# Block pairs of a two-layer DiT feed-forward: another layout of the weight tile, one split for A11 and A12, and another order of sums and products

## The chip, the core and the metric

The kernel runs on one core of one Trainium2 chip. The metric is the device time of one execution in microseconds. Each kernel is run several times and the median counts; differences are judged between kernels that ran on the same chip.

## The reference, cut to what matters

The reference is a two-layer diffusion transformer on 256 latent tokens and 256 context tokens with 1024 channels, all in float32. Layer 0 mixes with a short convolution, layer 1 with grouped-query attention. Around each mixer stand two gated feed-forwards. Each is this, on normalised and modulated tokens `h`, with a hidden size of 2816:

```python
def _swiglu(h, w13, w2):
    gte, up = jnp.split(h @ w13, 2, axis=-1)
    return (jax.nn.silu(gte) * up) @ w2
...
lat = lat + 0.5 * mod[:, 0, 2] * _swiglu(_modulate(lat, ...), ffn_w13[i, 0], ffn_w2[i, 0])
if cx is not None:
    cx = cx + 0.5 * modc[0, 2] * _swiglu(_modulate(cx, ...), ffn_w13[i, 0], ffn_w2[i, 0])
```

The first three of the four feed-forwards, (layer, place) = (0, 0), (0, 1) and (1, 0), run over both token streams; the last, (1, 1), over the latent stream alone. The change touches the product `h @ w13` of the first three.

## The kernel before

**Numbers.** TensorE works on float32r, and every operand is split into a high part and a low part. `split` (lines 107 to 109) does it with two operations: ScalarE copies the source into the high part with rounding (L108), VectorE subtracts that from the source for the low part (L109). `mm3` (lines 133 to 139) then adds three matmuls: high by high (L137), high weight by low token (L138), low weight by high token (L139).

**Tokens.** Activations lie transposed: 128 channels on the partitions, 512 columns, of which the first 256 are the latent and the last 256 the context tokens.

**Thirds.** The hidden size is cut into 22 tiles of 128, and these into thirds of 8, 7 and 7 (line 23). For each third, `ffn` (lines 777 to 886) makes the gated hidden tiles, and `project` (lines 584 to 643) multiplies them by `w2` and adds the result to the residual `x` (L567). The last two hidden tiles of a third are finished in between the first products of the projection.

**Pairs.** Most hidden tiles are computed by a `Pair` (lines 691 to 775), the Winograd form of Strassen's product: 7 block products in place of 8. The weight of one hidden tile is a 2 by 2 matrix of blocks of 128 rows by 512 columns: A11 and A12 are the gate's halves along the channels, A21 and A22 the up-projection's. The tokens are blocks B, by half of the channels and by stream. Sums of the B blocks are T1 to T4 (`Blocks.sums`, lines 412 to 432), made once for each feed-forward. Sums of the weights are made for each pair:

- S1 = A21 - A22, S2 = A11 - S1, S3 = A22 - S2 (which is A21 - A11), S4 = A12 - S2.

A product of one block, `prod` (lines 740 to 743), is 4 times `mm3`, so 12 matmuls of 256 columns. The seven are A11 with B11 and A12 with B21 (`head`), S1 with T1 (`five`), S2 with T2 and S4 with B22 (`six`), S3 with T3 (`seven`) and A22 with T4 (`four`). They are added up in two PSUM tiles, `p` and `q`. ScalarE copies `p` after A11 (L751), `q`'s second half after S1 (L757) and `p` after S2 (L761). VectorE then adds `sg` from `q` (L763), ScalarE applies Silu (L764), VectorE adds into `u` (L768), multiplies to the gate product `gm` (L774), and `gm` is split into the hidden tile `gh`, `gl`.

**Weights of a pair.** The DRAM tile `w13` has 2048 columns in four blocks of 512, in the order A21, A11, A22, A12 (lines 1432 and 1433). SyncE loads the last two blocks into the raw tile `r2`, and A11 into the second half of `r1`. GpSimd writes the negative of A22 into the first half of `r1` (L704), and a DMA issued by GpSimd adds A21 there (L707), so that `r1` holds S1 and A11. A11 is split from `r1` and A12 from `r2`, 512 columns each (L712). VectorE subtracts within `r1` (L726), and `keep` splits S1 and S2 at once, 1024 columns. Then A22 is split off by `split_far` (lines 111 to 115): two operations on ScalarE (L113, L114), and a DMA of GpSimd that adds the source to the negative high part. VectorE subtracts S2 from both halves of `r2` at once (L734, the wide sum), and S3 and S4 are split together.

**Buffers.** Raw tiles have 8 buffers (`wr`), split tiles 4 for each part (`wh`, `wl`), A22's parts 2 each (`w4h`, `w4l`).

**Order.** Nobody writes the order of these stages by hand (only the start of the kernel and the attention heads are): a scheduler orders the instructions of each engine from the order of the calls, the buffers and its own estimates. Between the pairs, VectorE also computes the modulation vectors, one row product of 1024 columns at a time (L178), doled out by `tick`. The products of the former pair's S3 and A22 come among those of the next pair. On TensorE the order in the middle of a third is A11, A12, S1, S3 of the former pair, S2, S4, A22 of the former pair. There are 56 pairs: 16 in (0, 0), whose first six tiles are computed plainly, and 20 each in (0, 1) and (1, 0), whose first two are.

Of the kernel before, what the change touches and what calls it, by code (L numbers as in the profile page):

```python
# [10 lines left out]
F32R = mybir.dt.float32r  # L11
# [5 lines left out]
P = 128  # L17
# [5 lines left out]
THIRDS = (8, 7, 7)  # L23

AS_IS = {(0, 0): range(3, 6), (0, 1): (), (1, 0): ()}

EARLY = 4
HEADS = 8
# [19 lines left out]
def hybrid_kernel(ctx: ExitStack, tc: tile.TileContext, a: dict, out: bass.AP):  # L48
# [68 lines left out]
    def half():  # L117

        return tuple(
            wp.tile([P, 1024], F32R, name=nm(t), tag=t, bufs=4) for t in ("wh", "wl")  # L120
        )
# [569 lines left out]
    class Pair:  # L691
# [6 lines left out]
        def __init__(self, src, h):  # L698
            self.h, self.w, self.src = h, {}, src
            r2 = load_raw(src[:, 1024:2048])  # L700
            r1 = wp.tile([P, 1024], F32, name=nm("wr"), tag="wr", bufs=8)
            nc.sync.dma_start(r1[:, T2:], src[:, T2:1024])

            nc.gpsimd.tensor_scalar(  # L704
                out=r1[:, :T2], in0=r2[:, :T2], scalar1=-1.0, scalar2=None, op0=ALU.mult
            )
            nc.gpsimd.dma_start(out=r1[:, :T2], in_=src[:, :T2], accum_op=ALU.add)  # L707
            self.raw = [r1, r2]
            ts = half()
            for i, key in enumerate(("A11", "A12")):  # L710
                self.w[key] = [t[:, i * T2 : i * T2 + T2] for t in ts]
                split(*self.w[key], self.raw[i][:, T2:])  # L712

        def keep(self, keys, part):
            hi, lo = half()
# [4 lines left out]
        def sums(self, n):  # L720

            r1, r2 = self.raw
            s1, s2 = r1[:, :T2], r1[:, T2:]
            tt = nc.vector.tensor_tensor
            if n == 0:
                tt(out=s2, in0=s2, in1=s1, op=ALU.subtract)  # L726
                self.keep(("S1", "S2"), r1)
                return
            self.w["A22"] = [
                wp.tile([P, T2], F32R, name=nm(t), tag=t, bufs=2) for t in ("w4h", "w4l")  # L730
            ]
            split_far(*self.w["A22"], r2[:, :T2], self.src[:, 1024 : 1024 + T2])
            v = lambda t: t.rearrange("p (a c) -> p a c", a=2)
            tt(  # L734
                out=v(r2), in0=v(r2), in1=s2.unsqueeze(1).to_broadcast([P, 2, T2]),
                op=ALU.subtract,
            )
            self.keep(("S3", "S4"), r2)

        def prod(self, ps, wk, hk, first=True):  # L740
            for k in range(4):
# [14 lines left out]
            self.gm = tp.tile([P, T2], F32, name=nm("gm"), tag="gm", bufs=3)  # L756
            nc.scalar.copy(self.gm[:, S:], self.q1)  # L757

        def six(self):
            self.prod(self.p, "S2", "T2", False)  # L760
            nc.scalar.copy(self.sg[:, S:], self.p)  # L761
            self.prod(self.q1, "S4", ("B", 1, 1), False)
            nc.vector.tensor_tensor(out=self.sg, in0=self.q, in1=self.sg, op=ALU.add)  # L763
            nc.scalar.activation(out=self.sg, in_=self.sg, func=AF.Silu)  # L764
# [12 lines left out]
    def ffn(l, b, h, tot, gate, tail, gs=(), ev=(0, 0), z=None):  # L777
        gs = list(gs)
        i0 = 0
        for t, n in enumerate(THIRDS):  # L780
            between = ()
            if tot == T2:
                heads = []
                if t == 0 and not gs:

                    w = [load_w(a["w13"][l, b, 0])]
                    gs = [new_pair("g") for _ in range(2)]
                    pp = [(psum("pg"), psum("pu")) for _ in range(2)]
                    w13_mm(pp[0], w[0], h, range(KT), 0, S)
                    flush()  # L790
                    w.append(load_w(a["w13"][l, b, 1]))
                    with tc.issue_after(every[-1]):
                        w13_mm(pp[1], w[1], h, range(KT), 0, S)
                    h.sums(0)
                    w13_mm(pp[0], w[0], h, range(KT), S, T2)
                    w13_post(pp[0], gs[0], 0, T2)
                    heads.append(Pair(a["w13"][l, b, 2], h))
                    h.sums(1)
                    heads[0].sums(0)
                    w13_mm(pp[1], w[1], h, range(KT), S, T2)  # L800
                    w13_post(pp[1], gs[1], 0, T2)
                    heads[0].head()
                    h.sums(2)
                    heads[0].sums(1)
                prev = None
                for i in range(len(gs), n):
                    if t == 0 and not heads and i in AS_IS[l, b]:
                        w = load_w(a["w13"][l, b, i])
                        pp = psum("pg"), psum("pu")
                        if prev:  # L810
                            prev.seven()
                        if "T1" not in h.t:
                            with tc.issue_after(rows["W1"]):
                                h.sums()
                        w13_mm(pp, w, h, range(4), 0, T2)
                        if prev:
                            gs.append(new_pair("g"))
                            prev.four(gs[-1])
                            prev = None
                        w13_mm(pp, w, h, range(4, KT), 0, T2)  # L820
                        gs.append(new_pair("g"))
                        tick(3, w13_post(pp, gs[-1], 0, T2))
                        continue
                    if heads:
                        pr = heads.pop(0)
                    else:
                        pr = Pair(a["w13"][l, b, i0 + i], h)
                        pr.sums(0)
                        pr.sums(1)
                        pr.head()  # L830
                    pr.five()
                    at = prev.seven().ins if prev else None
                    pr.six()
                    if prev:
                        gs.append(new_pair("g"))
                        prev.four(gs[-1])
                    prev = pr
                    if i:
                        tick(0.9, at)

                def last():
                    gs.append(new_pair("g"))
                    prev.four(gs[-1])

                between = (prev.seven, last) if prev else ()
            else:
                for i in range(n):
                    w = load_w(a["w13"][l, b, i0 + i])
                    gs.append(beside(gp.tile([P, T2], F32R, name=nm("gx"), tag="gh")))
                    pp = psum("pg"), psum("pu")  # L850
                    if i0 + i < EARLY:
                        for k in range(KT):
                            for j in range(2):
                                ps = pp[j][:, : z.w]
                                mm3(ps, w(at13(1 - j, k)), z.at(k), k == 0, k == KT - 1)
                            if i == 0 and k == KT // 2:
                                flush(1)
                        if i < 3:
                            flush(1)
                        early_post(pp, gs[i], z.ri)  # L860
                        tick(1)
                        continue
                    for j in range(2):
                        ws = [w(at13(1 - j, k)) for k in range(KT)]
                        mm_wide(pp[j], ws, [h.both(k) for k in range(KT)], True, True)
                    beside_post(pp, gs[i])
                    tick(1)
            i0 += n

            def ws2(m):  # L870
                src = a["w2a"][l, b, m // 2] if t == 0 else a["w2b"][l, b, t - 1, m // 2]
                o = (m % 2) * n * P
                raw = load_raw(src[:, o : o + n * P], n * P)
                hi, lo = half()
                split(hi[:, : n * P], lo[:, : n * P], raw[:, : n * P])
                return lambda k: (hi[:, k * P : k * P + P], lo[:, k * P : k * P + P])

            cur = gs
            end = t == len(THIRDS) - 1
            project(  # L880
                ws2,
                (lambda k, c0, c1: cur[k]) if tot == S
                else lambda k, c0, c1: (cur[k][0][:, c0:c1], cur[k][1][:, c0:c1]), n,
                gate, tail if end else None, tot, 2 if end and tot == T2 else 0, ev[end], between,
            )
            gs = []
# [525 lines left out]
def _layout(inp):  # L1412
# [17 lines left out]
    d["modb"] = f("mod_b").reshape(2, 72, P).transpose(2, 0, 1)  # L1430
    d["normg"] = f("norm_g").reshape(2, 3, KT, P).transpose(3, 0, 1, 2)
    w13 = f("ffn_w13").reshape(2, 2, 2, KT // 2, P, 2, NM, P)[:, :, :, :, :, ::-1]
    d["w13"] = w13.transpose(0, 1, 6, 4, 2, 5, 3, 7).reshape(2, 2, NM, P, 2048)
    w2 = f("ffn_w2").reshape(2, 2, NM, P, KT // 2, 2, P)
    w2 = w2.transpose(0, 1, 4, 3, 5, 2, 6)
    n0, n1 = THIRDS[:2]
# [53 lines left out]
```

## Time and profile before

| what | value |
|---|---|
| median of 3 runs | 1559.67 us |
| lowest and highest run | 1559.26 and 1561.86 us |
| span of the profiled execution, first to last instruction | 1558.7 us |
| VectorE operations, splits (L109) among them | 2030, 446 |
| ScalarE operations, splits (L108) among them | 1297, 446 |
| GpSimd operations | 187 |
| mean granted TensorE clock | 1.000 |

The time of the profiled execution is not listed apart from its span; the span lies 0.97 us below the median of the runs, which also hold what lies before the first and behind the last instruction. In the rows of a profile, PE is TensorE's matmul, PEld its weight load, DVE is VectorE, ACT ScalarE, POOL GpSimd and SP SyncE. A row of the timeline has start, length, engine, line, operation, tiles out and in, shape and count, and in brackets the idle time before it with what ended that. Rows that follow each other with the same line and tiles are merged, so the start of the next row tells how far apart operations start: an engine begins the next one before the former has fully ended.

### The profile page before, as it was taken

Reading aid. Unit: us, or ns where it says so; the run is one execution under the profiler, and the core shown is the slowest. Engines: PE = TensorE matmul, PEld = TensorE weight load, DVE = VectorE, ACT = ScalarE, POOL = GpSimd, SP = SyncE. Lnnn points to the kernel's source line nnn. Section 1 sums busy time; section 2 is a strip of 40 time slices with the busy share of each in tenths; the row PEclk is TensorE's granted clock in tenths of the full one; section 3 lists DMA queues with packets and bytes.
Section 4 is the critical chain, followed back from the end, with each engine's and each line's share of the span. In section 5 each row is a group of like instructions: output and inputs, shape, how many; then the busy total and the mean of one; then the engine's idle time right before and its main releaser. Section 6 shows DMA issues by size and latency. Waiting matters only on the chain.

```text
span 1558.7 us, 26399 instructions
## 1 busy us (share of the span) xinstructions
PE 1549.9 (99%) x10296; PEld 1422.0 (91%) x10296; DVE 1281.7 (82%) x2030; ACT 782.1 (50%) x1297; POOL 221.6 (14%) x187
## 2 busy tenths in 40 slices
PE   9999999999999999999999999999999999999999
PEld 7898998999888899989999899989999898998888
DVE  5788789799987588968978888968978887888676
ACT  5642553644423366436346466436346455774553
POOL 0012213200000112032042112022042002300000
PEclk9999999999999999999999999999999999999999
DMA  9567467465555425655656635655766843276562
GB/s 371 194 173 200 109 191 193 120 194 161 191 198 178 115 62 136 205 146 130 206 144 158 200 71 136 203 149 130 235 170 170 264 156 114 93 234 219 172 197 74
DMA packets 88253, 263.53 MB, mean 169 GB/s; under 512 B 10816, under 2 KB 12608, under 8 KB 88128
## 3 DMA queue, kind: packets, MB, share of 16 engines
q1 hardware_dynamic: 69408, 230.72, 45.8%
q0 software_dynamic: 16128, 29.37, 11.3%
q10 hardware_dynamic: 2592, 1.76, 0.4%
q8 instruction: 80, 1.31, 0.3%
q14 instruction: 45, 0.37, 0.1%
HBM read 259.45 MB, written 1.05 MB: 167 GB/s over the span
## 4 chain that ended last, share of the span: by engine, by line
PE 96%; DVE 2%; ACT 1%; issue 0%; POOL 0%; DVEq 0%; ACTq 0%; POOLq 0%
PE py L137 9%; PE py L138 9%; PE py L139 9%; PE p L137 7%; PE p L139 7%; PE p L138 7%; PE q L137 5%; PE q L139 5%; PE q L138 5%; PE py L145 2%; PE pu L145 2%; PE pg L145 2%; PE py L147 1%; PE pg L147 1%; PE pu L147 1%; PE pv L138 1%
## 5 line engine op out<-in xcount | busy, mean ns | idle before, releaser
L108 ACT ACTIVATE wh<-wr 128x1024 fp32r<-128x1024 f32 (+2 forms) x446 | 394.5, 912 | 325.2 <-PE py L138 126.1
L109 DVE TENSOR_TENSOR wl<-wr,wh 128x1024 fp32r<-128x1024 f32 (+2 forms) x446 | 456.6, 1048 | 85.9 <-ACT wh L108 66.8
L178 DVE CUSTOM_DVE_ANT_0 junk<-wr,scbc,modb 128x1024 bf16<-128x1024 f32 x213 | 274.7, 1290 | 11.4 <-DMA wr<-in_modT 9.3
L137 PE MATMUL py<-gh,wh 128*128 128x512 f32 (+1 forms) x570 | 213.5, 375 | 0.0
L138 PE MATMUL py<-gl,wh 128*128 128x512 f32 (+1 forms) x570 | 213.3, 374 | 0.0
L139 PE MATMUL py<-gh,wl 128*128 128x512 f32 (+1 forms) x570 | 213.2, 374 | 0.0
L704 POOL TENSOR_SCALAR wr<-wr 128x512 f32<-128x512 f32 x56 | 101.1, 1805 | 541.7 <-DMA wr<-in_w 286.3
L567 DVE SCALAR_TENSOR_TENSOR x<-py,mod,x 128x256 f32<-128x256 f32 x213 | 94.6, 479 | 65.6 <-PE py L139 54.3
L138 PE MATMUL p<-tl,wh 128*128 128x256 f32 x448 | 126.9, 283 | 0.0
L139 PE MATMUL p<-th,wl 128*128 128x256 f32 x448 | 126.9, 283 | 0.0
L137 PE MATMUL p<-th,wh 128*128 128x256 f32 x448 | 126.9, 283 | 0.0
L139 PEld LDWEIGHTS py<-gh,wl 128*128 128x128 f32 x570 | 107.4, 188 | 19.2
L137 PEld LDWEIGHTS py<-gh,wh 128*128 128x128 f32 x570 | 107.5, 189 | 18.3
L138 PEld LDWEIGHTS py<-gl,wh 128*128 128x128 f32 x570 | 107.5, 189 | 17.9
L115 POOL DMA_DIRECT2D w4l<-in_w x56 | 53.8, 960 | 445.7 <-ACT w4l L114 431.9
L137 PE MATMUL q<-bh,wh 128*128 128x256 f32 x320 | 90.8, 284 | 0.8 <-ACT wh L108 0.8
L139 PE MATMUL q<-bh,wl 128*128 128x256 f32 x320 | 90.8, 284 | 0.0
L138 PE MATMUL q<-bl,wh 128*128 128x256 f32 x320 | 90.6, 283 | 0.0
L137 PEld LDWEIGHTS p<-th,wh 128*128 128x128 f32 x448 | 86.0, 192 | 0.3
L138 PEld LDWEIGHTS p<-tl,wh 128*128 128x128 f32 x448 | 86.0, 192 | 0.3
L139 PEld LDWEIGHTS p<-th,wl 128*128 128x128 f32 x448 | 86.1, 192 | 0.0
L764 ACT ACTIVATE sg<-sg 128x512 f32<-128x512 f32 x56 | 35.4, 632 | 90.8 <-DVE sg L763 90.6
(305 smaller groups left out, 4081.2 us busy)
## 6 DMA issues: line engine op xcount, KB each, us to landing
wr<-in_w SPq DMA_DIRECT2D x120, 512.0 KB, 4.8
wr<-in_modT SPq DMA_DIRECT2D x117, 512.0 KB, 4.9
wr<-in_w2b SPq DMA_DIRECT2D x64, 448.0 KB, 4.0
wr<-in_w2a SPq DMA_DIRECT2D x32, 512.0 KB, 4.6
wr<-in_w SPq DMA_DIRECT2D x56, 256.0 KB, 3.9
wr<-in_w POOLq DMA_DIRECT2D x56, 256.0 KB, 5.8
w4l<-in_w POOLq DMA_DIRECT2D x56, 256.0 KB, 5.9
pm<-in_mod SPq DMA_DIRECT2D x16, 512.0 KB, 10.2
```

Source lines behind the costliest of these rows:

```text
L108: nc.scalar.activation(out=hi, in_=src, func=AF.Copy)
L109: return nc.vector.tensor_tensor(out=lo, in0=src, in1=hi.bitcast(F32), op=ALU.subtract)
L115: nc.gpsimd.dma_start(out=lo, in_=src, accum_op=ALU.add)
L137: nc.tensor.matmul(ps, wh, mh, start=first, stop=False, **kw)
L138: nc.tensor.matmul(ps, wh, ml, start=False, stop=False, **kw)
L139: nc.tensor.matmul(ps, wl, mh, start=False, stop=last, **kw)
L145: nc.tensor.matmul(ps, w[0], m[2], start=first and n == 0, stop=False)
L147: nc.tensor.matmul(ps[:, :S], w[1], m[0], start=False, stop=last and n == len(ms) - 1)
L178: nc.vector.tensor_tensor_reduce(out=junk, in0=raw, in1=scbc[:, v, :], scale=0.5 if ch in (2, 8) else 1.0, scalar=modb[:, l, col : col + 1 ...
L567: ins = nc.vector.scalar_tensor_tensor(out=x[:, m, s * S : s * S + S], in0=ps[:, o : o + S], scalar=g[:, m, s : s + 1], in1=x[:, m, s * S ...
L704: nc.gpsimd.tensor_scalar(out=r1[:, :T2], in0=r2[:, :T2], scalar1=-1.0, scalar2=None, op0=ALU.mult)
L764: nc.scalar.activation(out=self.sg, in_=self.sg, func=AF.Silu)
```

## The change

The four blocks of a pair's weight tile lie as A21, A22, A11, A12, for the tiles that are computed by pairs (the new table `SINGLE` tells from which tile on). So `r2` holds A11 and A12, which `keep` splits in one operation of 1024 columns. `r1` holds A21 - A11, which is S3, and A22. The first sum is now S2 = A22 - S3; A22 is split off before it, since the sum overwrites it; S3 and S2 are split together. The wide sum gives S1 = A11 - S2 and S4 = A12 - S2, and these are split together. The products are called in another order: S2 (`two`), S3 of the former pair, S1, A22 of the former pair, S4.

```diff
+SINGLE = {(0, 0): 6, (0, 1): 2, (1, 0): 2}
...
             nc.gpsimd.dma_start(out=r1[:, :T2], in_=src[:, :T2], accum_op=ALU.add)
             self.raw = [r1, r2]
-            ts = half()
-            for i, key in enumerate(("A11", "A12")):
-                self.w[key] = [t[:, i * T2 : i * T2 + T2] for t in ts]
-                split(*self.w[key], self.raw[i][:, T2:])
+            self.keep(("A11", "A12"), r2)
...
         def sums(self, n):
             r1, r2 = self.raw
-            s1, s2 = r1[:, :T2], r1[:, T2:]
+            s2 = r1[:, T2:]
             tt = nc.vector.tensor_tensor
             if n == 0:
-                tt(out=s2, in0=s2, in1=s1, op=ALU.subtract)
-                self.keep(("S1", "S2"), r1)
+                self.w["A22"] = [
+                    wp.tile([P, T2], F32R, name=nm(t), tag=t, bufs=2) for t in ("w4h", "w4l")
+                ]
+                split_far(*self.w["A22"], s2, self.src[:, T2:1024])
+                tt(out=s2, in0=s2, in1=r1[:, :T2], op=ALU.subtract)
+                self.keep(("S3", "S2"), r1)
                 return
-            self.w["A22"] = [
-                wp.tile([P, T2], F32R, name=nm(t), tag=t, bufs=2) for t in ("w4h", "w4l")
-            ]
-            split_far(*self.w["A22"], r2[:, :T2], self.src[:, 1024 : 1024 + T2])
             v = lambda t: t.rearrange("p (a c) -> p a c", a=2)
             tt(
                 out=v(r2), in0=v(r2), in1=s2.unsqueeze(1).to_broadcast([P, 2, T2]),
                 op=ALU.subtract,
             )
-            self.keep(("S3", "S4"), r2)
+            self.keep(("S1", "S4"), r2)
...
-        def six(self):
+        def two(self):
             self.prod(self.p, "S2", "T2", False)
             nc.scalar.copy(self.sg[:, S:], self.p)
+
+        def six(self):
             self.prod(self.q1, "S4", ("B", 1, 1), False)
...
+                    pr.two()
+                    at = prev.seven().ins if prev else None
                     pr.five()
-                    at = prev.seven().ins if prev else None
-                    pr.six()
                     if prev:
                         gs.append(new_pair("g"))
                         prev.four(gs[-1])
+                    pr.six()
...
-    d["w13"] = w13.transpose(0, 1, 6, 4, 2, 5, 3, 7).reshape(2, 2, NM, P, 2048)
+    w13 = w13.transpose(0, 1, 6, 4, 2, 5, 3, 7).reshape(2, 2, NM, P, 4, 512).copy()
+    for (l, b), n in SINGLE.items():
+        w13[l, b, n:] = w13[l, b, n:, :, (0, 2, 1, 3)].transpose(1, 2, 0, 3)
+    d["w13"] = w13.reshape(2, 2, NM, P, 2048)
```

## The prediction

> **What bounds the kernel now.** I read the page first: spans of the engines, the clock, and the chain that ended last.
>
> ```profile
> span 1558.7 us, 26399 instructions
> PE 1549.9 (99%) x10296; PEld 1422.0 (91%) x10296; DVE 1281.7 (82%) x2030; ACT 782.1 (50%) x1297; POOL 221.6 (14%) x187
> PEclk9999999999999999999999999999999999999999
> PE 96%; DVE 2%; ACT 1%; issue 0%; POOL 0%; DVEq 0%; ACTq 0%; POOLq 0%
> ```
>
> TensorE is busy for 99% of the span at full granted clock, and 96% of the chain is its own work. So time saved on VectorE or ScalarE is worth nothing where TensorE has its operands, and a new wait of TensorE costs its full length. Next I read a stretch inside the block pairs: busy time by engine, then the timeline of TensorE and of its weight loads.
>
> ```profile
> 602.00:642.00 40.00, 40.00 (x336) 40.00 (x335) 35.63 (x47) 26.11 (x44) 9.30 (x8) 1.00 0.64 170
> ```
>
> ```profile
> 602.00 0.28 PE L139 MATMUL p<-th,w4l 128*128 128x256 f32 x1
> 602.12 0.28 PE L137 MATMUL p<-bh,wh 128*128 128x256 f32 x1
> 602.36 0.28 PE L139 MATMUL p<-bh,wl 128*128 128x256 f32 x1
> 612.20 0.28 PE L137 MATMUL p<-bh,wh 128*128 128x256 f32 x1
> ```
>
> ```profile
> 602.25 0.19 PEld L139 LDWEIGHTS p<-bh,wl 128*128 128x128 f32 x1
> ```
>
> The columns of the first row are length, then busy us (and instructions) of PE, PEld, DVE, ACT, POOL, the clock, DMA. One pair is 7 products of 12 matmuls. From the first matmul of A11 at 602.12 to the next pair's at 612.20 are 84 matmuls in 10.08 us: 0.12 us each, with no gap. A weight load starts 0.11 us ahead of its matmul (602.25 for 602.36), so weights that land later than that stop TensorE.
>
> **Why nothing stops it today.** The same loop on VectorE, and the product that uses the weights:
>
> ```profile
> 618.07 0.68 DVE L726 TENSOR_TENSOR wr<-wr 128x512 f32<-128x512 f32 x1
> 620.21 1.22 DVE L109 TENSOR_TENSOR wl<-wr,wh 128x1024 fp32r<-128x1024 f32 x1
> 622.49 0.69 DVE L774 TENSOR_TENSOR gm<-sg,p 128x512 f32<-128x512 f32 x1 [0.46 <-PE p L139]
> 623.32 1.22 DVE L734 TENSOR_TENSOR wr<-wr,wr 128x1024 f32<-128x1024 f32 x1
> 624.46 0.68 DVE L109 TENSOR_TENSOR gl<-gm,gh 128x512 fp32r<-128x512 f32 x1
> ```
>
> ```profile
> 622.16 0.28 PE L139 MATMUL p<-th,w4l 128*128 128x256 f32 x1
> 625.16 0.28 PE L137 MATMUL q<-th,wh 128*128 128x256 f32 x1
> ```
>
> The S1, S2 weights of the pair whose A11 starts at 622.28 are complete at 621.43 and first used at 625.16: 3.7 us to spare. Their sum (L726) does not wait for the gate product: it runs before L774.
>
> **The change, part by part.** (1) The merged split. 56 times two splits of 512 columns become one of 1024.
>
> ```profile
> L109 DVE TENSOR_TENSOR wl<-wr,wh 128x512 fp32r<-128x512 f32 x132 | 86.0, 690 | 12.4 <-ACT wh L108 12.1
> L109 DVE TENSOR_TENSOR wl<-wr,wh 128x1024 fp32r<-128x1024 f32 x250 | 304.9, 1228 | 68.1 <-ACT wh L108 54.7 <-ACT sg L671 9.5 <-PE pu L147 3.1
> L108 ACT ACTIVATE wh<-wr 128x512 fp32r<-128x512 f32 x132 | 75.8, 620 | 29.8 <-PE py L138 24.4 <-PE q L138 2.5 <-PE pu L138 2.2
> L108 ACT ACTIVATE wh<-wr 128x1024 fp32r<-128x1024 f32 x250 | 263.1, 1058 | 231.2 <-PE py L138 72.8 <-DVE wr L726 51.7 <-PE p L138 27.6
> ```
>
> By these means VectorE saves 56 x (2 x 690 - 1228) ns = 8.5 us and ScalarE 56 x (2 x 620 - 1058) = 10.2 us. In the loop both had idle time (35.6 and 26.1 of 40 us busy), and TensorE hides all of it: 0.
>
> (2) The new order, in the loop. The instructions of the built changed program stand on VectorE, 38 times, as: GM (the gate product, old L774), the S2 sum, the wide sum, gl, SG (old L763), the low part of S3/S2, of S1/S4, of the next A11/A12, U (old L768), a modulation unit. On TensorE: A11, A12, two matmuls of S2, five of the former pair's S3, the other ten and seven, S1, A22 of the former pair, S4. The 38 are pairs 3 to 7 of six thirds with seven pairs and pairs 3 to 6 of the two with six; others have their sums made earlier, in the projection. GM waits for the former pair's A22 product, and the new pair's S2 weights now stand behind GM in VectorE's queue. That is the new chain; its rows:
>
> ```profile
> 642.14 0.69 DVE L763 TENSOR_TENSOR sg<-q,sg 128x512 f32<-128x512 f32 x1
> 642.74 0.68 DVE L774 TENSOR_TENSOR gm<-sg,p 128x512 f32<-128x512 f32 x1
> ```
>
> ```profile
> 674.82 0.68 DVE L726 TENSOR_TENSOR wr<-wr 128x512 f32<-128x512 f32 x1
> 675.60 1.23 DVE L734 TENSOR_TENSOR wr<-wr,wr 128x1024 f32<-128x1024 f32 x1
> ```
>
> ```profile
> 588.87 1.06 ACT L108 ACTIVATE wh<-wr 128x1024 fp32r<-128x1024 f32 x1 [0.37 <-DVE wr L734]
> 589.98 0.19 PEld L137 LDWEIGHTS q<-bh,wh 128*128 128x128 f32 x1 [0.66 <-ACT wh L108]
> ```
>
> Counted from the start of the last A22 matmul: 0.33 until GM starts (622.16 to 622.49); 0.60 to the next 512-column operation (642.14 to 642.74); S2 sum 0.78 to the wide sum, which needs its result (674.82 to 675.60); wide sum 1.14 (623.32 to 624.46); gl 0.60; SG 0.60; low part 1.22; 0.05 from an engine's end to the weight load (589.93 to 589.98). Sum 5.32 us. TensorE meanwhile has 12 + 24 + 2 + 5 matmuls; the 44th is S2's third, the first with a low part: 44 x 0.12 - 0.11 = 5.17. It is late by 0.15 us, each time: 38 x 0.15 = **5.7 us**. The lateness closes on itself: it delays the next A22 product as much.
>
> ScalarE's side is shorter: behind the wide sum (ended at 0.33 + 0.60 + 0.78 + 1.23 = 2.94) the high part of S1/S4, 1.06, the copy that frees A11's sum in PSUM for S2, 0.37, and 0.05 make 4.42, against 37 x 0.12 - 0.11 = 4.33 for S2's first matmul: late by 0.09, inside the 0.15. The S2 sum also waits, newly, for the high part of A22 on ScalarE, which waits for the second-last A22 matmul (two w4 buffers). At 0.62 us, as the 512-column row above, it runs from 0.20 to 0.82, and GM keeps VectorE until 0.93: 0. Were that cover gone, each 0.1 us would cost 38 x 0.1 = 3.8. Behind a late S2 sum stands VectorE's whole list, so both split halves; U, the next that TensorE waits for (at the former pair's A22), keeps some 0.7 us by the same rows.
>
> (3) Where a pair opens a third, S4 now follows S1 with only four matmuls between (before, S2's twelve). Both use one PSUM half, and ScalarE's copy stands between.
>
> ```profile
> 616.40 0.28 PE L139 MATMUL q<-th,wl 128*128 128x256 f32 x1
> 616.72 0.37 ACT L757 COPY gm<-q 128x256 f32<-128x256 f32 x1
> ```
>
> From S1's last matmul: 0.32 to the copy, 0.37, 0.05 = 0.74; S4's first load is due at 5 x 0.12 - 0.11 = 0.49. Late by 0.25, nine times: **2.2 us**.
>
> (4) Two stalls go. At the start of the second and third feed-forward VectorE is late with the wide sum, and S4 waits:
>
> ```profile
> 589.24 0.28 PE L139 MATMUL p<-th,wl 128*128 128x256 f32 x1
> 593.72 0.28 PE L137 MATMUL q<-bh,wh 128*128 128x256 f32 x1
> ```
>
> ```profile
> 939.66 0.28 PE L139 MATMUL p<-th,wl 128*128 128x256 f32 x1
> 944.08 0.28 PE L137 MATMUL q<-bh,wh 128*128 128x256 f32 x1
> ```
>
> 27 matmuls lie between, 3.24 us; they took 4.48 and 4.42: 1.24 + 1.18 = 2.4 us of stall. In the changed order the wide sum stands third from T1's low part on, not fourteenth. What is late next?
>
> ```profile
> 575.46 1.22 DVE L109 TENSOR_TENSOR tl<-hr,th 128x1024 fp32r<-128x1024 f32 x1
> ```
>
> ```profile
> 587.92 0.28 PE L137 MATMUL p<-th,wh 128*128 128x256 f32 x1
> ```
>
> From 575.46, eight operations of 1024 columns at 1.14, three of 512 at 0.60 and its own 1.22 end the low part of S1/S4 at 587.60. S1, now in the place that S2 has at 587.92, loads it at 587.92 + 0.24 - 0.11 = 588.05. So **-2.4 us**; one more 1024-column operation ahead would put 0.7 us of each stall back.
>
> (5) The queues. POOL and SP issue the same list; what moves is the release of raw tile r1, now behind the low part of S3/S2 (3.7 us into a pair's time, by the sum above).
>
> ```profile
> 611.94 2.27 POOL L704 TENSOR_SCALAR wr<-wr 128x512 f32<-128x512 f32 x1 [4.13 <-DVE sg L763]
> 614.62 0.89 POOL L707 DMA_DIRECT2D wr<-in_w  x1 [0.41 <-POOL wr L704]
> ```
>
> ```profile
> wr<-in_w POOLq DMA_DIRECT2D x56, 256.0 KB, 5.8
> ```
>
> POOL's negation, its issue and the landing take 2.3 + 0.9 + 5.8 = 9.0 us. The tile serves the pair two later, whose S2 sum starts 9.4 into the pair between: 10.1 - 3.7 + 9.4 = 15.8. With 6.8 us to spare, 0.
>
> Sum: 5.7 + 2.2 - 2.4 = 5.5 us on the profiled span of 1558.7, so 1564.2; the median of the runs shown, 1559.67, lies 0.97 above that span, so **1565.2 us**.
>
> **Bounds.** Lateness per loop, as an estimate from these rows: 0 if the dependent sum starts like an independent one (0.60, not 0.78), and 0.46 if the longest wide sum fell into every chain:
>
> ```profile
> L734 DVE TENSOR_TENSOR wr<-wr,wr x56: 1214/1225/1533, 85.4 to 1206.4; 128x1024 f32<-128x1024 f32 x56
> ```
>
> That is 1.53 against 1.22 (minimum, median and maximum in ns). I take 0.15, the sum of the common rows.
>
> **Rivals.** *Covered, and not slower.* If the wide sum follows the S2 sum as closely as an independent operation, the chain is 5.14 against 5.17, and no loop stalls: 1559.67 + 2.2 - 2.4 = 1559.5; with the copy in (3) hidden too, 1557.3. It decides at 0.15 us of a 5.3 us chain. Against it stands the pair at 674.82, where the second starts 0.10 after the first ends. The Trainium skill speaks for it ("VectorE: DVE Perf Modes", section "The DRAIN you can't avoid"): a semaphore between chained operations costs nothing extra. The trace disagrees by that pair's 0.18 us. Chance 0.22.
>
> *Heavier.* Lateness 0.46 per loop gives 17.5 + 2.2 - 2.4: 1577.0. For it speaks that the chain has no slack to take a stretched row; against it, that the median wide sum is within 0.01 us of the shortest, and that VectorE's loop, about 8.8 of 10.2 us by these rows, has its idle time ahead of GM, where extra work falls. Chance 0.12.
>
> *It does not do what it says.* The built program has 56 fewer splits on both engines; no chance left.
>
> **How the numbers follow.** Forecast 0.66, with its own range 1561.5 to 1570. The range of 1559.0 to 1574.0 takes in most of the covered case and stops short of the heavier one. 0.2% (3.1 us) is about what a measurement of this kernel can tell from no change. Faster than 1556.6 lies beyond even the best covered time: 0.03. Within 0.2%: 0.19 from covered and 0.03 from the forecast's low end, 0.22. Slower: 0.75.
>
> **What would show it.** In the changed profile: pairs 10.2 us apart in the loop; weight loads of p at S2 waiting for VectorE's low part some 38 times; nine waits of q at S4 for the ScalarE copy; no wait near 589 and 940. If pairs stay 10.08 us apart, step (2) is wrong; if they are 10.4 or more apart, its size is.

## The result, and the profile after

| what | before | after |
|---|---|---|
| median of the runs on the same chip | 1560.2 us (4 runs, 1559.26 to 1561.86) | 1578.03 us (4 runs, 1576.23 to 1579.72) |
| ratio, with its 95% interval | | 1.0114 (1.0102 to 1.0125) |
| span of the profiled execution | 1558.7 us | 1574.5 us |
| time of the profiled execution | | 1576.23 us |

The changed kernel is slower by 17.8 us, where 5.5 were forecast. The profiled execution is the fastest of the four; its span grew by 15.8 us, and that is what the trace can account for. All lines of the changed kernel up to the pairs have moved down by two (L109 is L111), the S2 sum is L729, the wide sum L733, the gate product GM L775. First the page: span, busy times, and the chain that ended last.

```profile
span 1574.5 us, 26263 instructions
...
PE 1560.4 (99%) x10296; PEld 1428.1 (91%) x10296; DVE 1279.4 (81%) x1974; ACT 775.3 (49%) x1241; POOL 227.1 (14%) x187
...
PE 90%; DVE 3%; DMA 3%; ACT 1%; issue 1%; POOL 1%; ACTq 0%; SPq 0%; POOLq 0%; DVEq 0%
```

The 56 splits are gone from VectorE (1974 operations for 2030) and ScalarE (1241 for 1297), and TensorE still reads 99%. But the chain is TensorE's own work for 90% only, not 96%, and 3% of it are now a DMA, which had no share at all. So something that waits for a transfer has come onto the path. The waits of TensorE's weight loads and of VectorE (columns: who waited, for whom, us in total, times, longest) say where:

```profile
PEld ss L277 <- DVE acc L268: 4.4, 2, 3.6
PEld p L139 <- ACT sg L750: 3.0, 8, 1.1
...
PEld q L139 <- ACT gm L756: 1.7, 9, 0.2
```

```profile
DVE gm L775 <- PE p L141: 49.0, 38, 2.4
...
DVE wr L729 <- DMA wr<-in_w: 26.1, 9, 5.1
```

The nine waits of `q` for ScalarE's copy and the 38 of GM for the A22 product were forecast. The two waits of the RMS sum (`ss`, L277) and the 26.1 us in which VectorE stood at an S2 sum for a transfer were not. Before, VectorE stood there 4.5 us in two places:

```profile
DVE wr L726 <- DMA wr<-in_w: 4.5, 2, 3.5
```

**Where the 15.8 us are.** Matmuls of one form start at a usual distance (0.12 us for 256 columns, 0.227 for 512). I summed from TensorE's records, place by place, by how much they start farther apart. The same sums of four experiments below stand beside it:

| us beyond the usual distance | before | after | e1_heads | e2_w4h | e7_fill15 | e8_all2 |
|---|---|---|---|---|---|---|
| first 60 us | 13.8 | 12.4 | 13.5 | 13.4 | 12.9 | 13.7 |
| pairs, products into `p` | 0.4 | 8.5 | 10.0 | 1.0 | 8.0 | 2.1 |
| pairs, products into `q` | 1.8 | 2.1 | 2.1 | 2.2 | 2.1 | 0.7 |
| ahead of the second feed-forward, 545 to 575 us | 0.1 | 6.3 | 0.1 | 5.7 | 0.9 | 0.1 |
| ahead of the third, 895 to 926 us | 1.4 | 3.1 | 2.3 | 4.0 | 3.1 | 1.6 |
| rest up to 1240 us | 0.7 | 1.5 | 0.7 | 5.5 | 0.7 | 0.7 |
| behind 1240 us | 4.4 | 4.4 | 4.3 | 4.3 | 5.0 | 4.4 |
| sum | 22.6 | 38.3 | 33.0 | 36.2 | 32.7 | 23.2 |

(In e7_fill15 come 3.4 us of dummy matmuls on top.) The difference of the first two sums is 15.7 of the span's 15.8 us: +8.0 in the pairs' loops, +0.3 at S4, and +7.9 ahead of the second and third feed-forward, about which the prediction said nothing; 0.8 came in small pieces, and the first 60 us, which the change does not touch, were 1.4 us shorter in this execution (all rounded).

**The part that was not foreseen.** VectorE in the changed kernel, at the end of the projection ahead of the second feed-forward (start, length, engine, line, operation, tiles; in brackets the idle time before it and what ended that):

```profile
550.51 0.76 DVE L268 TENSOR_TENSOR acc<-acc,sq 128x256 f32<-128x256 f32 x2
556.35 0.69 DVE L729 TENSOR_TENSOR wr<-wr 128x512 f32<-128x512 f32 x1 [5.08 <-DMA wr<-in_w]
556.96 0.48 DVE L569 SCALAR_TENSOR_TENSOR x<-py,mod,x 128x256 f32<-128x256 f32 x1
557.91 0.43 DVE L268 TENSOR_TENSOR acc<-acc,sq 128x256 f32<-128x256 f32 x1 [0.48 <-ACT sq L260]
```

```profile
548.77 1.49 POOL L706 TENSOR_SCALAR wr<-wr 128x512 f32<-128x512 f32 x1 [6.74 <-DVE wl L111]
550.66 0.91 POOL L709 DMA_DIRECT2D wr<-in_w  x1 [0.41 <-POOL wr L706]
```

```profile
558.40 0.59 PE L277 MATMUL ss<-ones,acc 128*128 128x1 f32 x2 [3.37 <-DVE acc L268]
```

Read it from the S2 sum at 556.35. It belongs to the second pair of the next feed-forward. VectorE came to it at 551.27 and stood for 5.08 us, since the transfer that completes raw tile `r1` was issued by GpSimd only at 550.66. Behind it in VectorE's order stand the last residual `x` (L569) and the square sum `acc` (L268), which have nothing to do with the weights. TensorE needs `acc` for the RMS sum, and stood for 3.4 us. Before, no L726 runs between 535 and 566 us; the first head pair's sum ran at 578.94, behind the norm, and stood for no transfer there. Stretches of the changed kernel's TensorE from there (length, busy us and count of PE, PEld, DVE, ACT, POOL, then the granted clock, DMA share and GB/s):

```profile
555.00:558.00 3.00, 0.02 (x1) 0.00 (x0) 1.17 (x3) 0.42 (x1) 0.00 (x0) 0.84 0.66 113
558.00:560.00 2.00, 1.35 (x6) 1.27 (x6) 0.74 (x2) 0.42 (x1) 0.00 (x0) 0.50 0.00 0
560.00:562.00 2.00, 2.00 (x11) 2.00 (x11) 0.17 (x1) 0.26 (x1) 0.00 (x0) 0.50 0.00 0
562.00:564.00 2.00, 2.00 (x11) 2.00 (x11) 1.15 (x3) 0.64 (x2) 0.00 (x0) 0.53 0.00 0
564.00:566.00 2.00, 2.00 (x19) 2.00 (x18) 2.00 (x6) 2.00 (x6) 0.00 (x0) 1.00 0.00 0
```

The busy share says 2.00 of 2 us from 560 to 564, but only 11 matmuls ran in each stretch, against 19 from 564 on: the granted clock had dropped to 0.50. So the stop cost 3.5 us, 0.5 at the second square sum, and 2.3 more at half pace.

### The profile page after: what moved, and what is told of

It is laid out like the page before. It is cut to its first block, busy times and chain, and to the rows that moved or that the text cites. A ratio compares the mean times of both kernels' runs of the same rounds, so it can differ in the third digit from the quotient of the medians.

```text
span 1574.5 us, 26263 instructions
## 1 busy us (share of the span) xinstructions
PE 1560.4 (99%) x10296; PEld 1428.1 (91%) x10296; DVE 1279.4 (81%) x1974; ACT 775.3 (49%) x1241; POOL 227.1 (14%) x187
## 4 chain that ended last, share of the span: by engine, by line
PE 90%; DVE 3%; DMA 3%; ACT 1%; issue 1%; POOL 1%; ACTq 0%; SPq 0%; POOLq 0%; DVEq 0%
PE py L139 7%; PE py L140 7%; PE py L141 7%; PE p L139 7%; PE p L141 7%; PE p L140 7%; PE q L139 5%; PE q L140 5%; PE q L141 5%; DMA wr<-in_w 3%; PE py L147 2%; PE pu L147 2%; PE pg L147 2%; PE py L149 1%; PE pg L149 1%
## 5 line engine op out<-in xcount | busy, mean ns | idle before, releaser
L111 DVE TENSOR_TENSOR wl<-wr,wh 128x1024 fp32r<-128x1024 f32 (+2 forms) x390 | 453.1, 1184 | 58.4 <-ACT wh L110 39.4
L706 POOL TENSOR_SCALAR wr<-wr 128x512 f32<-128x512 f32 x56 | 105.0, 1874 | 756.6 <-DMA wr<-in_w 353.9
L569 DVE SCALAR_TENSOR_TENSOR x<-py,mod,x 128x256 f32<-128x256 f32 x213 | 94.4, 478 | 41.7 <-PE py L141 30.5
L141 PEld LDWEIGHTS p<-th,wl 128*128 128x128 f32 x448 | 82.6, 191 | 1.4
L775 DVE TENSOR_TENSOR gm<-sg,p 128x512 f32<-128x512 f32 x56 | 38.5, 687 | 49.0 <-PE p L141 49.0
```

What stands on the lines that cost most here:

```text
L111: return nc.vector.tensor_tensor(out=lo, in0=src, in1=hi.bitcast(F32), op=ALU.subtract)
L141: nc.tensor.matmul(ps, wl, mh, start=False, stop=last, **kw)
L569: ins = nc.vector.scalar_tensor_tensor(out=x[:, m, s * S : s * S + S], in0=ps[:, o : o + S], scalar=g[:, m, s : s + 1], in1=x[:, m, s * S ...
L706: nc.gpsimd.tensor_scalar(out=r1[:, :T2], in0=r2[:, :T2], scalar1=-1.0, scalar2=None, op0=ALU.mult)
L775: nc.vector.tensor_tensor(out=self.gm, in0=self.sg, in1=self.u, op=ALU.mult)
```

## The experiments

All are edits of the changed kernel. Each was run on one chip together with the kernel before, whose median there was 1559.9 to 1560.1 us; the ratios are to that. The theory: three separate losses, the head sums' wait in VectorE's order (7.9 us), the chain through GM in the loop (8.0), the copy ahead of S4 (2.2). The rivals: another cause of the late RMS sum, a VectorE that is too full in any order, a clock that drops for another reason.

### e1_heads: the head pairs' S2 sums behind the norm

`recs` holds the reciprocals of the norm, one for each stream. On the engines exactly these four sums move, and nothing else.

```diff
             if n == 0:
...
-                tt(out=s2, in0=s2, in1=r1[:, :T2], op=ALU.subtract)
+                with tc.issue_after(at) if at else nullcontext():
+                    self.sum = tt(out=s2, in0=s2, in1=r1[:, :T2], op=ALU.subtract).ins
...
-                    heads[0].sums(0)
+                    heads[0].sums(0, recs[-2])
...
-                        pr.sums(0)
+                        pr.sums(0, recs[-1] if t == 0 and i == 3 and (l, b) != (0, 0) else None)
```

> The changed kernel, with the first weight sum (S2) of the first two pairs of the second and third feed-forward put behind the two reciprocals of the norm on VectorE, out of the projection before it; no other instruction moves. Theory H (VectorE stands at these sums and waits for the transfer that completes raw tile r1, and the residual and the square sums queue behind it): the 3.5 us wait of the RMS sum near 555 and the half-speed stretch behind it go, and most of the wait near 913; of the changed kernel's 1578 us some 7.5 go, so 1570.5 (1569 to 1572). Rival (the RMS sum is late because the squares or the transfers of that moment are slow): the wait stays where it is, 1577 to 1579.

Measured: 1570.09 us (5 runs, 1567.67 to 1571.98), ratio to before 1.0063 (1.0050 to 1.0075). That is 7.9 us less than the changed kernel. VectorE at the same place:

```profile
551.76 0.48 DVE L569 SCALAR_TENSOR_TENSOR x<-py,mod,x 128x256 f32<-128x256 f32 x1
552.89 0.43 DVE L268 TENSOR_TENSOR acc<-acc,sq 128x256 f32<-128x256 f32 x1 [0.64 <-ACT sq L260]
...
557.17 0.17 DVE L286 RECIPROCAL ri<-rs 128x2 f32<-128x2 f32 x1 [2.04 <-ACT rs L282]
557.25 0.69 DVE L730 TENSOR_TENSOR wr<-wr 128x512 f32<-128x512 f32 x1
```

The square sum ends at 553.3 in place of 558.3, the S2 sum (now L730) fits behind the reciprocal without any wait, and TensorE loses 0.1 us from 545 to 575 in place of 6.3. (The spans differ by 5.3 us only: the changed kernel's profiled execution is its fastest, and 1.5 us came in the pairs, with one wait of 1.9 us from 1158.3 to 1160.3, ahead of which VectorE stands at the first two S2 sums of the last third for their transfers.) The transfers were left as they were, so it was the place of the sum in VectorE's order, and not a slow transfer by itself. The S1 weights were not late afterwards either: what the prediction feared behind the norm did not happen.

### e2_w4h: a third buffer for A22's high part

```diff
-                    wp.tile([P, T2], F32R, name=nm(t), tag=t, bufs=2) for t in ("w4h", "w4l")
+                    wp.tile([P, T2], F32R, name=nm(t), tag=t, bufs=n) for t, n in (("w4h", 3), ("w4l", 2))
```

(The edit also gives GM's method an argument that no call uses.)

> The changed kernel with three buffers in place of two for the high part of A22, so that the S2 sum of the next pair no longer waits for the former pair's A22 product. Theory L (the chain A22 product, GM, S2 sum, wide sum, low part of S3/S2 is what stops TensorE by 0.17 us in each of 38 loops, and by up to 0.4 in one loop of each third): pairs come 10.08 us apart again and some 8 us go, 1570 (1568.5 to 1571.5). Rival (VectorE is simply too full in the loop, in whichever order): pairs stay at 10.2 us and the time at 1577 to 1579.

Measured: 1574.98 us (4 runs, 1574.11 to 1575.10), ratio 1.0094 (1.0080 to 1.0107); a miss in the time, 3.1 us where 8 were expected. The place by place sums show why. In the loop it came as expected: `p` loses 1.0 us in place of 8.5, and VectorE's waits for the A22 product have nearly gone, from 38 to 3:

```profile
DVE gm L776 <- PE p L141: 2.0, 3, 0.7
```

A pair takes the usual time again:

```profile
628.83 0.28 PE L139 MATMUL p<-bh,wh 128*128 128x256 f32 x1
...
638.90 0.28 PE L139 MATMUL p<-bh,wh 128*128 128x256 f32 x1
```

10.07 us lie between the starts of two pairs. So VectorE is not too full: the order was the limit. (The edit lets the scheduler change the order in many places on every engine, so it tests the order as a whole and not one wait. In the loop of the changed kernel at 628, A22's rounding on ScalarE, which needs the buffer, ended at 628.75, and VectorE went from GM to the S2 sum at 628.85: both held that sum, nearly equally.) But with a buffer more the scheduler pulled further S2 sums forward, at the head of the third feed-forward too, and these now stand ahead of the norm's scaling (L307):

```profile
930.60 0.69 DVE L729 TENSOR_TENSOR wr<-wr 128x512 f32<-128x512 f32 x1 [2.73 <-issue]
931.21 1.65 DVE L307 SCALAR_TENSOR_TENSOR t<-x,A,ss 128x256 f32<-128x256 f32 x4
```

```profile
933.37 0.39 PE L139 MATMUL pg<-bh,wh 128*128 128x256 f32 x1 [1.06 <-ACT bh L110]
...
935.18 0.58 PE L140 MATMUL pg<-bl,wh 128*128 128x256 f32 x1 [1.07 <-DVE bl L111]
```

TensorE waited there twice for the scaled tokens and ran at half pace behind it. This is the loss that e1_heads removes, in a new place. The line "rest" of the table holds it: 5.5 us in place of 1.5, so 4.0 of the 7.5 us won in the pairs were given back.

### e3_third: S1 before S2 where a pair opens a third

```diff
-                    pr.two()
-                    at = prev.seven().ins if prev else None
-                    pr.five()
+                    if prev or (t == 0 and i == 2):
+                        pr.two()
+                        at = prev.seven().ins if prev else None
+                        pr.five()
+                    else:
+                        pr.five()
+                        pr.two()
+                        at = None
```

> The changed kernel with S1 before S2 for the pair that opens a third, in seven of the nine places (not at the heads of the second and third feed-forward), so that S2's twelve matmuls stand between S1 and S4. Theory T (S4 waits 0.25 us for ScalarE's copy of S1): seven of nine such stalls go, 1.75 us, 1576.3. Rival (S1's weights are not ready twelve matmuls earlier): new waits of S1 take their place, 1578 or more.

Measured: 1575.23 us (4 runs, 1574.89 to 1577.75), ratio 1.0100 (1.0086 to 1.0114). The intervals of this kernel and of the changed one overlap, so the time alone does not decide. The trace does: of nine waits of S4 for the copy, seven are gone. At the two left (598.3 and 953.0 us) two matmuls start 0.145 and 0.10 us late, 0.25 in all, as the prediction had worked it out. One new wait came, 0.43 us at 1165: there the S1 weights were not ready twelve matmuls earlier. It stands where the changed kernel lost 1.1 us for S2.

### e4_split2: the merged split undone

```diff
-            self.keep(("A11", "A12"), r2)
+            ts = half()
+            for i, key in enumerate(("A11", "A12")):
+                self.w[key] = [t[:, i * T2 : i * T2 + T2] for t in ts]
+                split(*self.w[key], r2[:, i * T2 : i * T2 + T2])
```

> The changed kernel with the merged split of A11 and A12 undone: two splits of 512 columns each, 56 more operations on VectorE and on ScalarE, 8.5 and 10.2 us by the rows of before. Theory S (the idle time ahead of GM and beside the products takes them): 1577 to 1580, so the merged split was worth about nothing. Rival (the loop is bound by VectorE's work): 0.15 us more in each of 38 loops, 5.7 us, 1583.7.

Measured: 1579.77 us (4 runs, 1577.58 to 1581.04), ratio 1.0123 (1.0107 to 1.0138), against 1.0114 (1.0102 to 1.0125) with the merged split. The groups of VectorE's split, first of the changed kernel, then of this one (line, operation, shapes, count, busy us, mean ns, idle time before):

```profile
L111 DVE TENSOR_TENSOR wl<-wr,wh 128x1024 fp32r<-128x1024 f32 x306 | 370.9, 1237 | 52.4 <-ACT wh L110 39.2 <-ACT sg L673 9.5 <-PE pu L149 3.1
...
L111 DVE TENSOR_TENSOR wl<-wr,wh 128x512 fp32r<-128x512 f32 x20 | 13.2, 685 | 0.5 <-ACT wh L110 0.2
```

```profile
L111 DVE TENSOR_TENSOR wl<-wr,wh 128x1024 fp32r<-128x1024 f32 x250 | 300.3, 1220 | 43.7 <-ACT wh L110 30.7 <-ACT sg L673 9.5 <-PE pu L149 3.1
...
L111 DVE TENSOR_TENSOR wl<-wr,wh 128x512 fp32r<-128x512 f32 x132 | 90.6, 723 | 5.7 <-ACT wh L110 5.3
```

384.1 us with the merged split and 390.9 without: 6.8 us of VectorE's time. The medians of the kernels differ by 1.7 us, and their intervals overlap, so no difference is shown. The rival's 5.7 us lie outside the interval.

### e5_fill and e7_fill15: dummy matmuls in the stop

The RMS sum's tile has unused columns. Matmuls of ones by ones are written there ahead of the sum in the norm of the second feed-forward: 30 in e5_fill, 15 in e7_fill15. Nothing uses their results, and no other instruction moves.

```diff
+        calls.append(s)
+        if len(calls) == 5:
+            with tc.issue_after(place_[0]):
+                for _ in range(15):
+                    f = nc.tensor.matmul(pq[:, 300 : 300 + P], ones, ones, start=True, stop=True)
```

> The changed kernel with 30 dummy matmuls of 128 columns (0.111 us each, 3.3 us) ahead of the RMS sum of the second feed-forward's norm, where TensorE stands still for 3.5 us near 555; their results are used by nothing, and no other instruction moves. Theory K (the idle stretch itself drops the granted clock, and the matmuls behind it then run at half pace): the wait for the square sum stays (VectorE is as late as before), the spacing behind it stays 0.12 us, and of the 6.3 us lost there some 2.3 go: 1575.7 (1574.5 to 1577). Rival (the half pace comes from the tiny matmuls, their weights or the late norm): half pace stays, 1577.5 to 1580.

Measured: 1577.28 us (4 runs, 1575.61 to 1578.12), ratio 1.0107 (1.0092 to 1.0123). The granted clock stayed at 1.00 there, but the dummies ran too long, 6.86 us for a stop of 3.5, so the time says nothing:

```profile
556.32 6.86 PE L281 MATMUL ss<-ones 128*128 128x128 f32 x60
```

> As e5_fill, with 15 dummy matmuls in place of 30. The trace of e5_fill showed that each is run as two (60 rows, 6.7 us), so that it overran the wait of 3.5 us by some 3 us, while the granted clock stayed at 1.00. Theory K: 30 rows of 0.111 us fill the wait and no more; spacing behind it 0.12 us at clock 1.00, and of the 6.3 us lost at this place some 2.3 go: 1575.7 (1574.5 to 1577). Rival (the half pace has another cause and went in e5_fill only because the norm came 3 us later): half pace is back, 1577.5 to 1580.

Measured: 1576.25 us (4 runs, 1573.96 to 1577.63), ratio 1.0107 (1.0091 to 1.0122). The runs scatter by more than the effect, so the time does not settle it: two of them had a mean granted clock of 1.000 (1573.96 and 1574.91 us), the other two of 0.997 and 0.999 (1577.58 and 1577.63), so their clock dropped somewhere that no trace shows. The trace, of the first, does settle it for this place. The dummies, then the same stretches as above from 558, in e7_fill15:

```profile
555.57 3.51 PE L281 MATMUL ss<-ones 128*128 128x128 f32 x30
```

```profile
558.00:560.00 2.00, 1.54 (x13) 1.30 (x12) 0.90 (x3) 0.83 (x2) 0.00 (x0) 1.00 0.00 0
560.00:562.00 2.00, 2.00 (x17) 1.94 (x18) 0.17 (x1) 0.26 (x1) 0.00 (x0) 1.00 0.00 0
562.00:564.00 2.00, 2.00 (x19) 2.00 (x19) 1.98 (x6) 1.46 (x4) 0.00 (x0) 1.00 0.04 8
```

The wait for VectorE is as long, but the matmuls behind it run at clock 1.00, 17 and 19 in 2 us in place of 11 (560 to 564). This place loses 0.9 us beside the dummies' 3.4, in place of 6.3: 2.0 us were the half pace.

### e6_all and e8_all2: the repairs together

e6_all joins e1_heads, e2_w4h and e3_third, with the third head pair's S2 sum anchored too (behind the first token sum, VectorE's operation for T1). e8_all2 takes up the two new waits that e6_all's trace showed; the diff is the step between them. `h.late` is VectorE's last token sum, for T4 (the fourth; the expectation counts it as the fifth).

```diff
-                        pr.sums(0, {3: recs[-1], 4: h.first}.get(i) if t == 0 and (l, b) != (0, 0) else None)
+                        pr.sums(0, {3: recs[-1], 4: h.late}.get(i) if t == 0 and (l, b) != (0, 0) else None)
...
-                    if prev or (t == 0 and i == 2):
+                    if prev or (t == 0 and i == 2) or (l, t) == (1, 2):
```

> The changed kernel with the three repairs together: the first weight sums of the first three pairs of the second and third feed-forward behind the norm's reciprocals and the first token sum, three buffers for A22's high part, S1 before S2 in seven of nine thirds. Theory (the three losses are separate: 7.9 at the heads, 8.0 in the loops less what is left in single loops, 1.8 at the thirds' starts): the stalls left are those of before without its two at the heads, 1559.5 (1557.5 to 1562), the same as before within what can be told. Rival (VectorE's work, put behind the heads and pulled ahead in the loops, collides in a new place): 1563 or more, with a new wait in the trace.

Measured: 1562.62 us (11 runs, 1561.91 to 1564.58), ratio 1.0018 (1.0009 to 1.0027). Just outside the theory's range: the repairs' prices add up, but the rival has a part in it. Two waits of TensorE are new, at 575.85 (1.27 us, for tokens; VectorE stood 1.43 us at an S2 sum ahead of them) and at 1152.17 (1.24 us, for S1's low part):

```profile
572.84 0.69 DVE L730 TENSOR_TENSOR wr<-wr 128x512 f32<-128x512 f32 x1 [1.43 <-DMA wr<-in_w]
```

> As e6_all, with the two new waits of its trace removed: the third head pair's S2 sum one step later, behind the fifth token sum (in e6_all it held VectorE 1.43 us for a transfer, and TensorE waited 1.4 us at 574.6), and S2 before S1 again in the last third of the third feed-forward (S1 waited 1.4 us at 1150.9). Theory (the price of the three losses is separate and nothing else is late): 1562.6 less 2.8 less 0.3, 1559.6 (1558 to 1561), the same as before. Rival (the saved 8.5 us of VectorE show once nothing is late): under 1557.

Measured: 1560.70 us (11 runs, 1559.16 to 1563.59), ratio 1.0005 (0.9996 to 1.0014): the time of before within what can be told, 17 us below the changed kernel. It lies in the theory's range, and the rival (under 1557) fell. Of the two waits the first is gone. The second only changed its place: S2, ahead of S1 again, now waits there for ScalarE's copy of `p`, so 1.9 us went in all where 3.1 were expected.

```profile
1151.16 0.39 PE L139 MATMUL p<-th,wh 128*128 128x256 f32 x1 [1.12 <-ACT sg L751]
```

Its page:

```profile
span 1559.3 us, 26303 instructions
...
PE 1549.6 (99%) x10296; PEld 1422.1 (91%) x10296; DVE 1275.2 (82%) x1974; ACT 779.4 (50%) x1241; POOL 229.6 (15%) x187
...
PE 96%; DVE 1%; ACT 1%; issue 0%; DMA 0%; POOL 0%; ACTq 0%; DVEq 0%; POOLq 0%
```

The chain is TensorE's for 96% again, as before. VectorE and ScalarE have 56 operations fewer than before, and the kernel is not faster for it. Of what is left of stalls (23.2 us against 22.6), 18.1 us lie in the first 60 us and behind 1240, where the change does nothing, and 2.3 in two waits for ScalarE's copy of `p`, at 614.9 and at 1151.2. No version here beats the kernel before.

## Why the prediction was wrong, step by step

The sign was right, the size was not: 5.5 us more were forecast, and 17.8 came. One large loss was missing from the sum, and a few small ones.

**(1) The merged split, 0: right.** Its busy time fell by 6.8 us on VectorE (8.5 by the means of before; the mean of the splits of 1024 columns rose from 1228 to 1237 ns), TensorE hides it, and e4_split2 and e8_all2 show no gain that can be told.

**(2) The loop, 5.7 us: the term was right, but not all that the loop lost.** The rows of one loop in the changed kernel:

```profile
628.25 0.69 DVE L775 TENSOR_TENSOR gm<-sg,p 128x512 f32<-128x512 f32 x1 [1.25 <-PE p L141]
628.85 0.69 DVE L729 TENSOR_TENSOR wr<-wr 128x512 f32<-128x512 f32 x1
629.64 1.23 DVE L733 TENSOR_TENSOR wr<-wr,wr 128x1024 f32<-128x1024 f32 x1
```

VectorE's order is the one forecast. In the steady loops S2's second matmul starts 0.075 us late, behind ScalarE's copy of `p`, and the one that follows its first low part 0.095, behind VectorE; the next ones follow a little closer. Pairs lie 10.21 to 10.23 us apart there (mean of 22: 10.225), as "10.2 us" said, against 10.08 before: 0.145 us each, and 38 x 0.145 = 5.5, where 5.7 was forecast. The rest of the 8.0 us had no term in the sum. Eight loops, in seven of the thirds, lie 10.33 to 10.66 us apart, which is 2.0 us more in all; in them TensorE waits longer for ScalarE's copy of `p` (L750). The opening of the last third of the third feed-forward lost 1.1 us, see (4). And 0.6 us that the kernel before lost in `p` near 590 and 941 are gone. The bound of 0.46 per loop, which the rival "heavier" took everywhere, was passed in two loops only (0.51 and 0.58). That rival's 1577.0 lies near the measured time by luck: the loops lost 7.5 us (5.5 and 2.0) of the 17.5 that it took, and the heads of (4) made up most of the difference. In one of the eight loops a likely reason can be read:

```profile
618.38 0.92 DVE L729 TENSOR_TENSOR wr<-wr 128x512 f32<-128x512 f32 x1
```

```profile
618.15 1.48 POOL L706 TENSOR_SCALAR wr<-wr 128x512 f32<-128x512 f32 x1 [1.84 <-DMA wr<-in_w]
```

The S2 sum took 0.92 us in place of 0.69 while GpSimd's negation ran beside it. It is so in seven of the eight loops: the S2 sum took 0.78 to 0.92 us, or the wide sum 1.44 to 1.66, with a negation beside it. The sums of the changed kernel that had none beside them, 48 S2 sums and 45 wide sums, took at most 0.69 and 1.23 us. But not every sum beside a negation was stretched, and no experiment moved the negations, so that they are the cause is not shown. (In the eighth loop, at 190.6, the wide sum started 0.47 us late.) The rival "covered" fell: the two dependent sums lie 0.10 us apart here too, in the median of 43 such pairs.

**(3) The openings of the thirds, 2.2 us: right**, nine times 0.25 (the nine places in the changed kernel's trace; e3_third removes seven).

**(4) The failed step.** The two stalls at S4 are gone, as forecast. But the step then asked "What is late next?" and looked only behind T1's low part, where the earlier wide sum is a gain. Step (2) had already noted that the other pairs' sums are "made earlier, in the projection", and gave that no price. There the first sum stands, in VectorE's fixed order, ahead of the residual and the square sum, and it waits for a transfer. It cost 3.5 us of standing still, 0.5 at the second square sum and 2.3 at half pace, and 1.7 in the same way ahead of the third feed-forward, where VectorE stood 4.07 us at the sum at 908.93: with what before lost there, 6.2 + 1.7 = 7.9 us. e1_heads gives 7.0 of them back in these places, and 7.9 in the median.

The same happened once more, in small. At the last third of the third feed-forward VectorE stood 3.89 and 2.58 us at the first two S2 sums for their transfers (before 3.51 at one of them), the splits came late, and S2's first matmul waited for ScalarE's copy, which stood behind them:

```profile
1165.46 0.39 PE L139 MATMUL p<-th,wh 128*128 128x256 f32 x1 [0.85 <-ACT sg L750]
```

This opening lost 1.1 us with the restart, and 1.4 to 2.0 in e1_heads, e6_all and e8_all2: none of the repairs touches it, so its cause is read from the rows and not tried.

**(5) The queues, 0: right in the loop, not asked at the heads.** The 6.8 us to spare were worked out for the loop, where `r1` is loaded two pairs ahead. At a head GpSimd's list starts only when the projection's splits release the raw tiles (548.77, released by L111); the issue started at 550.66, and the sum at 556.35, when its transfer had landed. VectorE was there at 551.27. What lets the sum go so early is read from the code and was not tried: in the kernel before it overwrites A11 and must follow both of A11's split operations; now it overwrites A22, and follows only ScalarE's rounding.

With 7.9 us for the heads and 8.0 for the loop, the sum would have been 8.0 + 0.3 + 7.9 = 16.2 on the span, against 15.8 measured (less 1.4 us in the first 60 us, and 0.8 more in small pieces). The range of 1559.0 to 1574.0 was too narrow on its upper side for want of a rival "a sum that was made late is now made early, and blocks its engine".

## What to carry to other kernels

An operation that moves forward in an in-order queue is a risk as well as a gain: for each one, look up when its last operand lands at the new place, and which unrelated work stands behind it there. Time saved on an engine that TensorE hides is worth nothing, and a slack worked out in the steady loop says nothing of the first turns after another stage. A stop of TensorE may cost more than its length, since the clock can drop with it.

## What was not expected of the hardware

**The clock after a stop.** In the stop of 3.5 us the granted clock fell to 0.50 at 557.05, while TensorE still stood, and rose at 563.88; with dummy matmuls in the stop it stayed at 1.00. The Trainium skill has this rule ("TensorE: Matmul & The Clock Gate", Part 1, "The HAM clock gate"): the rate halves after an idle window of about 3.4 us and comes back after as long a busy one, and the window runs freely. The traces agree with the length and with the free run: in the changed kernel the clock changes at 557.05, 563.88, 915.45 and 918.86 us, which are 2, 103 and 1 steps of 3.413 us apart, and each execution's steps lie elsewhere. They do not agree with a window that must be idle: in the step ahead of 557.05 TensorE was busy for 1.38 of 3.41 us. Ahead of the third feed-forward waits of 0.67 and 0.46 us were enough. First the waits, then two steps of the changed kernel:

```profile
913.60 0.38 PE L277 MATMUL ss<-ones,acc 128*128 128x1 f32 x2 [0.67 <-DVE acc L268]
914.44 0.38 PE L277 MATMUL ss<-ones,sq 128*128 128x1 f32 x2 [0.46 <-ACT sq L260]
```

```profile
912.04:915.45 3.41, 2.28 (x18) 2.00 (x17) 1.90 (x5) 0.98 (x3) 0.85 (x1) 1.00 0.75 184
915.46:918.86 3.40, 3.40 (x19) 3.40 (x18) 1.86 (x6) 1.03 (x3) 0.00 (x0) 0.50 0.28 51
```

In e7_fill15 the waits at the same place were 0.78 and 0.46 us, no shorter, and the clock stayed:

```profile
912.16 0.38 PE L284 MATMUL ss<-ones,acc 128*128 128x1 f32 x2 [0.78 <-DVE acc L270]
913.00 0.38 PE L284 MATMUL ss<-ones,sq 128*128 128x1 f32 x2 [0.46 <-ACT sq L262]
```

```profile
909.59:913.00 3.41, 2.17 (x18) 1.89 (x17) 2.39 (x6) 0.83 (x2) 0.89 (x1) 1.00 0.74 159
913.00:916.41 3.41, 3.41 (x28) 3.35 (x29) 1.44 (x5) 1.03 (x3) 0.00 (x0) 1.00 0.48 94
```

There a step ends at 913.00 (counted back in 193 steps of 3.413 us from the clock's last change, at 1571.78), inside the stretch with few matmuls; in the changed kernel the whole of that stretch lies within one step. An estimate from all ten traces puts a number to it. Take each matmul at its usual distance and those of one column as nothing. Behind the first 60 us, the ten steps at clock 1.00 that were followed by half pace were then filled for at most 0.38 of their length, and all other steps at clock 1.00 for at least 0.43. So a stop of little more than a microsecond can, but need not, cost half pace, by where it falls in these steps. This is read from the traces; no experiment set the start of the steps.

**Two matmuls for one.** A dummy of 128 columns with plain float32 operands appears as two matmuls (30 written, 60 in the trace, 6.86 us).
